# A two-layer decoder of mixers: gated linear attention ahead of latent attention, and the rotary table made between the two

## The chip, the core and the metric

The kernel runs on one core of one Trainium2 chip. The metric is the device time of one execution in microseconds. An execution has five engines with an instruction stream each: TensorE (PE, matrix products; PEld is its weight load), VectorE (DVE), ScalarE (ACT), GpSimd (POOL) and SyncE (SP, which issues DMAs). Matrix products write to PSUM, everything else lies in SBUF.

## The reference

Two layers act on x with 256 tokens of 1024 features. The first third of a layer is the part that the change touches: four mixers run on the same normalised input, and their outputs are gated and merged.

```python
def mixer_block(h, positions, w_in, ...):
    zin = h @ w_in
    (cq, ckv, kpe, sg_uv, gq, gk, gv, g_lr, g_og,
     dq, dk, dv, da, db, dz, gates) = jnp.split(zin, splits, axis=-1)
    o_a = mla_branch(cq, ckv, kpe, positions, mla_norm_q, mla_norm_kv, mla_w_uq, mla_w_ukv)
    o_b = spatial_gating_branch(sg_uv, sg_ln_g, sg_ln_b, sg_w, sg_b)
    o_c = gla_branch(gq, gk, gv, g_lr, g_og, gla_w_gate, gla_b_gate, gla_norm)
    o_d = deltanet_branch(dq, dk, dv, da, db, dz, dn_conv, dn_a_log, dn_dt_bias, dn_norm)
    proj = jnp.einsum('bsnw,nwd->bsnd', branches, w_branch)
    gate = jax.nn.sigmoid(gates).reshape(b, s, N_BRANCH, D_MODEL)
    return jnp.sum(gate * proj, axis=2) @ w_out
```

`mla_branch` (latent attention, MLA) normalises a compressed query and key, projects both up by weights of its own, rotates 32 of the features by the cosines and sines of the positions (the rotary table), and runs causal softmax attention with four heads. `gla_branch` (gated linear attention, GLA) weights the products of queries and keys by exponentials of summed log gates. `spatial_gating_branch` is gMLP, `deltanet_branch` DeltaNet. GLA and DeltaNet end in the same way: a norm of the heads' outputs, times a gate. After the mixers, a layer has cross-attention with a memory and an MLP, which the change leaves alone.

## The kernel before

**Weights.** All weights come as one stream from HBM in the order of use. A *half* is 128 x 1024 numbers. `half()` (line 174) takes the next one from a raw tile `wr` (three of them, filled by SP's DMAs with two halves each) and splits it into a high part `wh`, rounded to fp32r, on ACT (L191) and the remainder `wl` on DVE (L194). There are four tiles each for `wh` and `wl`. `mm3` (L198, L199, L200) makes one product out of three matmuls: high by high, low by high, high by low. A half feeds 24 matmuls of 256 columns, in groups of eight products that accumulate in a PSUM tile `g` (three of these).

**Order.** A list scheduler of the tile framework simulates the five engines when the kernel is built and fixes each engine's instruction stream. Among instructions that could start, the one earlier in the program goes first. The weight splits count as 200 places earlier than they stand, and statistics and the like as more. So the order in which the program text issues the mixers sets which DVE work competes with which split.

**The mixers.** In a layer the program first runs the input projection: five pairs of output blocks for DeltaNet's inputs and shared ones, then `soft_gates` and `conv` of DeltaNet, then `zin_rest` (four more pairs, and gMLP's and GLA's values by token). In layer 0, `rope_table` (L394) is called between `conv` and `zin_rest`. It loads the positions and the mask of GLA, multiplies the positions by frequencies on GpSimd (L400 to L404), takes off multiples of two pi on DVE (three times L410), folds (L412 on GpSimd, L414 and L415 on DVE) and takes the sine on ACT (L416) into a constant tile `cs`. Layer 1 uses the same `cs`.

Then two generators run in turns, a step of each at a time: `dn()`, which is DeltaNet's system, solve and output, and `others()`, which is gMLP, MLA and GLA in that order. Each `yield` in them ends a step. The program text of the gates (32 halves, their results in tiles `gt`) follows behind, and PE gets gate matmuls wherever the mixers leave room.

MLA (L897 to L1003) uses two halves of the weight stream of its own: the query's up-projection, 24 matmuls whose results are multiplied by `cs` on DVE (`qm`, L929), and the key's and value's. Its norm's root is some dozen steps of 0.15 us on DVE (`rsqrt`, L271 to L283). GLA (L789 to L893) makes differences `dd` of the summed gates at seven levels (DVE, L819 to L826), clamps them on GpSimd (L827), takes exponentials on ACT, multiplies 4 x 7 times a query by one of these (`qt`, DVE, L861), has PE multiply the result with keys (L866), and picks the masked entries into `sc` (DVE). Its values then enter by L885 to L888.

`head_out` (L754) is the end of DeltaNet and of GLA. It squares the output on ACT, sums on PE (L763), gates on ACT and DVE (L764 to L766), takes a reciprocal root of 14 steps on DVE, copies it out to `rb` on ACT (L779), transposes that on PE (L783), and multiplies (L784). It reads the gate into the tile of the squares, so the gate follows the sums.

**Tiles.** Mixers and others share a list of equal pieces in SBUF. `new` takes the piece that has been free longest, `rel` gives it back; a tile thereby waits for the last reader of the piece's former tile. The first four gate pairs have tiles of their own; from the fifth on (`m >= 4`) `gates` takes pieces.

Of the kernel before, what the change touches and what calls it, by code (L numbers as in the profile page):

```python
# [64 lines left out]
def decoder(ctx: ExitStack, tc: tile.TileContext, ws, xn_d, xt_d, mem_d, pos_d, fin_d, par_d, cst_d, msk_d, out_d):  # L65
# [29 lines left out]
    def new(dt=F32, shape=(P, 2, T), name="a"):  # L95
        assert free, "no piece left: " + str(sorted(n for _, _, n in owner.values()))
        i = free.pop(0)
        t = ap.tile(list(shape), dt, tag=f"pc{i}", name=nm(name))
        owner[id(t)] = (i, t, name)
        return t  # L100

    def rel(*ts):
        for t in ts:
            if isinstance(t, (list, tuple)):
                rel(*t)
                continue
            free.append(owner.pop(id(t))[0])
# [4 lines left out]
    def small2(a, b, name):  # L112
        return sp.tile([P, a, b], F32, tag=name, name=nm(name))

    def bank(shape=(P, 2, T)):
        return pp.tile(list(shape), F32, tag="s", name=nm("ps"))
# [3 lines left out]
    msk = cp.tile([P, M_N], I32, name="msk")  # L120
# [14 lines left out]
    def later(*a):  # L135

        tc.keep_in_program_order(nc.sync.dma_start(*a))
# [133 lines left out]
    def rsqrt(src, n, scale, eps, name):  # L271
        x = small(n, name + "x")
        y = small(n, name + "y")
        t = small(n, name + "t")
        V.tensor_scalar(x, src, scale, eps, op0=ALU.mult, op1=ALU.add)
        V.tensor_scalar(y.bitcast(I32), x.bitcast(I32), 1, None, op0=ALU.logical_shift_right)
        V.tensor_scalar(y.bitcast(I32), y.bitcast(I32), -1, MAGIC, op0=ALU.mult, op1=ALU.add)
        V.tensor_scalar(x, x, -0.5, None, op0=ALU.mult)
        for _ in range(3):
            V.tensor_tensor(t, y, y, op=ALU.mult)  # L280
            V.tensor_tensor(t, t, x, op=ALU.mult)
            V.scalar_tensor_tensor(y, t, 1.5, y, op0=ALU.add, op1=ALU.mult)
        return y  # L283
# [106 lines left out]
    def bc2(row, n=2):  # L390
        return row.unsqueeze(1).to_broadcast([P, n, T])


    def rope_table():  # L394
        posi = new(dt=I32, shape=(P, T), name="posi")
        later(posi, pos_d)
        later(msk, msk_d)
        ang, n = new(shape=(P, T)), new(shape=(P, T))
        q = slice(64, 128)
        G.tensor_copy(ang[q], posi[q])  # L400
        G.tensor_scalar(ang[q], ang[q], cst[q, C_FREQ : C_FREQ + 1], None, op0=ALU.mult)
        G.tensor_scalar(n[q], ang[q], float(1.0 / (2 * np.pi)), None, op0=ALU.mult)
        G.tensor_scalar(n[q], n[q], 12582912.0, None, op0=ALU.add)
        G.tensor_scalar(n[q], n[q], -12582912.0, None, op0=ALU.add)  # L404
        rest = 2 * np.pi
        for bits in (8, 8, 24):
            e = int(np.floor(np.log2(rest))) - bits + 1
            c = float(np.floor(rest / 2.0**e) * 2.0**e)
            rest -= c
            V.scalar_tensor_tensor(ang[q], n[q], -c, ang[q], op0=ALU.mult, op1=ALU.add)  # L410
        pi = float(np.nextafter(np.float32(np.pi), np.float32(0)))
        G.tensor_scalar(ang[q], ang[q], pi, -pi, op0=ALU.min, op1=ALU.max)  # L412
        c = slice(64, 96)
        V.scalar_tensor_tensor(ang[c], ang[c], -1.0, ang[c], op0=ALU.mult, op1=ALU.min)  # L414
        V.tensor_scalar(ang[c], ang[c], float(np.pi / 2), None, op0=ALU.add)  # L415
        S.activation(cs[q], ang[q], AF.Sin)  # L416
        G.memset(cs[0:64], 1.0)
        rel(posi, ang, n)

    def hsl(h):  # L420
        return slice(64 * (h % 2), 64 * (h % 2) + 64)
# [3 lines left out]
    def bch(a, shape=W4):  # L425
        return a.unsqueeze(1).to_broadcast(list(shape))
# [11 lines left out]
    def layer(l):  # L438
        pr = cp.tile([P, PC_N], F32, tag="par", name=nm("par"))

        def col(o, n=1):
            return pr[:, o : o + n]
# [7 lines left out]
        def out_branch(n, src):  # L450
            brh[n], brl[n] = new(F32R, name="brh"), new(F32R, name="brl")
            S.copy(brh[n], src)
            V.tensor_tensor(brl[n], src, brh[n].bitcast(F32), op=ALU.subtract)
# [284 lines left out]
        def zin_rest():  # L738
            def ev_rest(p, parts):
                ps = parts[0][1]  # L740
                t = new(name=("og", "dz", "cq", "su")[p])
                V.tensor_tensor(t, ps, bc2(R.rrow), op=ALU.mult)
                setattr(R, ("og", "dz", "cq", "su")[p], t)

            gemm(X, XL, 8, 4, ev_rest)
            R.zs = []

            def ev_tok(t, ps):
                z = new(name="zs", shape=(P, 512))
                S.activation(z, ps, AF.Copy, scale=R.rs[:, t : t + 1])  # L750
                R.zs.append(z)

            weights("tok")
            gemm_tok(X, XL, 8, ev_tok)  # L754
# [250 lines left out]
        def gmlp():  # L1005
            su, zs = R.su, R.zs

            def gelu2(z, shape):

                w = new(name="ge", shape=shape)  # L1010
                S.activation(w, z, AF.Square)
                G.tensor_scalar(w, w, 0.044715, 1.0, op0=ALU.mult, op1=ALU.add)
                G.tensor_tensor(w, w, z, op=ALU.mult)
                S.activation(w, w, AF.Tanh, scale=float(np.sqrt(2.0 / np.pi)))
                V.scalar_tensor_tensor(w, w, 1.0, z, op0=ALU.add, op1=ALU.mult)
                return w

            bst, bag = small2(2, 6, "bst"), small2(2, 2, "bag")
            vl = new(name="vl")
            gv = [gelu2(zs[t][:, 0:256], (P, T)) for t in range(2)]  # L1020
            for t in range(2):
                V.bn_stats(bst[:, t], gv[t])
                V.bn_aggr(bag[:, t], bst[:, t])
            rv = rsqrt(bag[:, :, 1], 2, 0.25, EPS, "ln")
            V.tensor_scalar(rv, rv, 0.5, None, op0=ALU.mult)
            for t in range(2):
                V.tensor_scalar(vl[:, t], gv[t], bag[:, t, 0:1], rv[:, t : t + 1], op0=ALU.subtract, op1=ALU.mult)
            rel(gv)
            G.tensor_tensor(vl, vl, bc2(col(PC_LNG, T)), op=ALU.mult)
            G.tensor_tensor(vl, vl, bc2(col(PC_LNB, T)), op=ALU.add)  # L1030
            yield
            wm = new(name="wm", shape=W4)
            G.tensor_tensor(wm, col(PC_WS, 512).rearrange("p (a b) -> p a b", a=4), bch(tri), op=ALU.mult)
            gu = gelu2(su, (P, 2, T))
            yield
            mp = bank()
            for h in range(4):
                for t in range(2):
                    PE.matmul(mp[hsl(h), h // 2, 128 * t : 128 * t + 128], vl[:, t, 64 * h : 64 * h + 64], wm[:, h], start=True, stop=True)
            mx = new(name="mx")  # L1040
            for t in range(2):
                s = slice(128 * t, 128 * t + 128)
                V.tensor_tensor(mx[:, :, s], mp[:, :, s], col(PC_BS, 256).rearrange("p (a b) -> p a b", a=2), op=ALU.add)
            V.scalar_tensor_tensor(mx, mx, 0.5, gu, op0=ALU.mult, op1=ALU.mult)
            out_branch(1, mx)
            rel(mx, gu, su, vl, wm)
            yield
# [6 lines left out]

        def others():
            yield from gmlp()
            yield from mla()
            yield from gla()

        soft_gates()  # L1060
        conv()
        if l == 0:
            rope_table()
        zin_rest()

        if l == 0:
# [3 lines left out]
        for j in range(4):  # L1070
# [7 lines left out]
            rel(t)  # L1078

        run = [dn(), others()]  # L1080
        while run:
            for gen in list(run):
# [208 lines left out]
    for l in range(NL):  # L1291
        layer(l)
# [177 lines left out]
```

## Time and profile before

| | before |
|---|---|
| median of 3 runs | 1099.93 us (1099.71 to 1100.56) |
| profiled execution, its own time | 1101.14 us |
| its span in the trace | 1098.5 us |
| mean granted TensorE clock | 0.996 |
| instructions | 20696 |

The span is the time from the first to the last instruction in the trace, and the remaining 2.6 us of the profiled execution lie around it. A group of instructions is printed as the line, the engine, the operation, the tile written and those read, the shape and the count; behind the bar stand the busy time in us and the mean of one in ns, then idle time of the engine ahead of it and what ended that. A wait is printed as who waited for whom, with the sum in us, the number of times and the longest. Layer 0's input projection runs until about 105 us of the span, its mixers until about 235 and its gates to the end of the mixers' third; layer 1's mixers begin at about 630 us.

### The profile page before, as it was taken

Reading aid. Unit: us, or ns where it says so; the run is one execution under the profiler, and the core shown is the slowest. Engines: PE = TensorE matmul, PEld = TensorE weight load, DVE = VectorE, ACT = ScalarE, POOL = GpSimd, SP = SyncE. Lnnn points to the kernel's source line nnn. Section 1 sums busy time; section 2 is a strip of 40 time slices with the busy share of each in tenths; the row PEclk is TensorE's granted clock in tenths of the full one; section 3 lists DMA queues with packets and bytes.
Section 4 is the critical chain, followed back from the end, with each engine's and each line's share of the span. In section 5 each row is a group of like instructions: output and inputs, shape, how many; then the busy total and the mean of one; then the engine's idle time right before and its main releaser. Section 6 shows DMA issues by size and latency. Waiting matters only on the chain.

```text
span 1098.5 us, 20696 instructions
## 1 busy us (share of the span) xinstructions
PE 1074.4 (98%) x8494; PEld 1032.4 (94%) x8494; DVE 812.5 (74%) x1419; ACT 584.2 (53%) x875; POOL 194.6 (18%) x170
## 2 busy tenths in 40 slices
PE   8989999999999999999999999999999999999996
PEld 8979998899998999999999899999999899999885
DVE  6999857779866876655679997686797768665454
ACT  6565554554645655544454746554455555555342
POOL 6234005108200200000101420320351001010000
PEclk9999999999999999999999999999999999999999
DMA  9442523354544455555545444244445345554551
GB/s 354 163 179 111 204 104 121 110 193 156 191 153 154 154 192 192 192 192 193 192 183 192 155 154 154 103 150 151 174 177 204 122 152 193 186 194 177 192 192 38
DMA packets 28319, 185.13 MB, mean 169 GB/s; under 512 B 3392, under 2 KB 3648, under 8 KB 6976
## 3 DMA queue, kind: packets, MB, share of 16 engines
q1 hardware_dynamic: 26208, 179.09, 44.9%
q10 hardware_dynamic: 2016, 4.72, 1.3%
q8 instruction: 66, 1.08, 0.4%
q14 instruction: 29, 0.24, 0.1%
HBM read 182.75 MB, written 1.05 MB: 167 GB/s over the span
## 4 chain that ended last, share of the span: by engine, by line
PE 86%; DVE 8%; ACT 2%; DMA 2%; issue 1%; POOL 0%; DVEq 0%; ACTq 0%
PE g L198 25%; PE g L199 25%; PE g L200 25%; DVE wl L194 2%; DMA mr<-memt 1%; PE ps L198 1%; PE ps L199 1%; PE ps L200 1%; ACT wh L191 1%; PE ps L666 1%; PE ps L662 1%; DVE cv L539 1%; DVE qt L861 0%; DMA wr<-ws 0%; PE ps L972 0%
## 5 line engine op out<-in xcount | busy, mean ns | idle before, releaser
L194 DVE TENSOR_TENSOR wl<-wr,wh 128x1024 fp32r<-128x1024 f32 (+1 forms) x337 | 416.9, 1239 | 187.8 <-ACT wh L191 186.6
L191 ACT ACTIVATE wh<-wr 128x1024 fp32r<-128x1024 f32 (+1 forms) x337 | 355.1, 1057 | 344.3 <-PE g L199 238.8
L200 PE MATMUL g<-hh,wl 128*128 128x256 f32 x1152 | 325.1, 282 | 3.5 <-DVE wl L194 3.5
L198 PE MATMUL g<-hh,wh 128*128 128x256 f32 x1152 | 323.8, 282 | 1.9 <-ACT gt L1097 1.4
L199 PE MATMUL g<-hl,wh 128*128 128x256 f32 x1152 | 322.9, 280 | 0.0
L200 PEld LDWEIGHTS g<-hh,wl 128*128 128x128 f32 x1152 | 216.5, 188 | 5.5 <-DVE wl L194 4.5
L198 PEld LDWEIGHTS g<-hh,wh 128*128 128x128 f32 x1152 | 216.5, 188 | 3.1 <-ACT gt L1097 1.8
L199 PEld LDWEIGHTS g<-hl,wh 128*128 128x128 f32 x1152 | 217.3, 189 | 0.4 <-issue 0.2
L338 POOL TENSOR_TENSOR sq<-sq,sq 128x512 f32<-128x512 f32 x14 | 21.2, 1513 | 350.5 <-ACT sq L330 350.3
L198 PE MATMUL g<-xh,wh 128*128 128x256 f32 x272 | 75.5, 281 | 2.0 <-ACT xh L311 2.0
L199 PE MATMUL g<-xl,wh 128*128 128x256 f32 x272 | 75.8, 281 | 0.0
L200 PE MATMUL g<-xh,wl 128*128 128x256 f32 x272 | 74.9, 280 | 0.0
L198 PE MATMUL g<-ah,wh 128*128 128x256 f32 x256 | 70.7, 276 | 0.0
L199 PE MATMUL g<-al,wh 128*128 128x256 f32 x256 | 70.7, 276 | 0.0
L200 PE MATMUL g<-ah,wl 128*128 128x256 f32 x256 | 70.7, 276 | 0.0
L198 PEld LDWEIGHTS g<-xh,wh 128*128 128x128 f32 x272 | 51.3, 190 | 2.4 <-ACT xh L311 2.4
L1113 POOL TENSOR_TENSOR gt<-gt,gt 128x512 f32<-128x512 f32 x16 | 35.6, 2228 | 91.0 <-DVE gt L1112 90.0
L199 PEld LDWEIGHTS g<-xl,wh 128*128 128x128 f32 x272 | 51.2, 189 | 0.1
L200 PEld LDWEIGHTS g<-xh,wl 128*128 128x128 f32 x272 | 51.0, 189 | 0.0
L200 PE MATMUL g<-wh,al 128*128 128x512 f32 x128 | 49.5, 389 | 0.0
L199 PE MATMUL g<-wl,ah 128*128 128x512 f32 x128 | 49.5, 389 | 0.0
L198 PE MATMUL g<-wh,ah 128*128 128x512 f32 x128 | 49.4, 390 | 0.0
(500 smaller groups left out, 2332.6 us busy)
## 6 DMA issues: line engine op xcount, KB each, us to landing
wr<-ws SPq DMA_DIRECT2D x166, 1024.0 KB, 4.8
wr<-ws ACTq DMA_DIRECT2D x4, 512.0 KB, 7.6
mr<-memt ACTq DMA_DIRECT2D x8, 256.0 KB, 4.5
par<-par SPq DMA_DIRECT2D x2, 778.0 KB, 7.0
x<-xt SPq DMA_DIRECT2D x3, 256.0 KB, 7.7
cst<-cst SPq DMA_DIRECT2D x1, 588.0 KB, 8.7
gf<-fin SPq DMA_DIRECT2D x2, 256.0 KB, 5.3
yt<-yg ACTq DMA_DIRECT2D x2, 256.0 KB, 2.5
```

What stands on the lines that cost most here:

```text
L191: i = S.activation(wh[:, p], r[:, p], AF.Copy)
L194: V.tensor_tensor(wl[:, p], r[:, p], wh[:, p].bitcast(F32), op=ALU.subtract)
L198: PE.matmul(out, ah, bh, start=start, stop=False)
L199: PE.matmul(out, ah, bl, start=False, stop=False)
L200: PE.matmul(out, al, bh, start=False, stop=stop)
L338: G.tensor_tensor(acc, acc, sq, op=ALU.add)
L539: V.scalar_tensor_tensor(cv[:, c, d], zc[p][:, c, 0 : T - 3 + k], col(o + k), cv[:, c, d], op0=ALU.mult, op1=ALU.add)
L662: PE.matmul(xp[:, h], M[:, h], Tm[:, h], start=True, stop=True)
L666: PE.matmul(up[:, h], X[t][:, h], U[:, h], start=True, stop=True)
L1113: G.tensor_tensor(gt[m][0], gt[m][0], gt[m][1], op=ALU.add)
```

## The change

GLA comes ahead of MLA in `others()`, in both layers. In layer 0 the rotary table is made between the two; the mask, which `rope_table` also loaded, is loaded where the table was made before. No step is added or left out.

```diff
@@ -394,7 +394,6 @@
     def rope_table():
         posi = new(dt=I32, shape=(P, T), name="posi")
         later(posi, pos_d)
-        later(msk, msk_d)
         ang, n = new(shape=(P, T)), new(shape=(P, T))
@@ -1054,13 +1053,15 @@
         def others():
             yield from gmlp()
+            yield from gla()
+            if l == 0:
+                rope_table()
             yield from mla()
-            yield from gla()
 
         soft_gates()
         conv()
         if l == 0:
-            rope_table()
+            later(msk, msk_d)
         zin_rest()
```

Lines from 398 to 1056 have numbers smaller by one in the changed kernel.

On DVE, between the splits of two neighbouring gate halves of layer 0 while DeltaNet's system is being solved (`w` is the solve, `rmt` MLA's norm, `wl` a split), there stood before:

```order
L194 TENSOR_TENSOR wl_1967<-wr_1936,wh_1966 128x1024
L642 TENSOR_TENSOR w_1111<-w_1111 128x8x13
L281 TENSOR_TENSOR rmt_1143<-rmt_1143,rmx_1141 128x4
L194 TENSOR_TENSOR wl_2000<-wr_1997,wh_1999 128x1024
L640 STREAM_SHUFFLE w_1111<-w_1111 128x8x12
L282 SCALAR_TENSOR_TENSOR rmy_1142<-rmt_1143,rmy_1142 128x4
```

And now, between the same two splits:

```order
L194 TENSOR_TENSOR wl_1967<-wr_1936,wh_1966 128x1024
L641 TENSOR_TENSOR w_1094<-w_1094 128x8x14
L452 TENSOR_TENSOR brl_1091<-mx_1086,brh_1090 128x512
L860 TENSOR_TENSOR qt_1240<-dd_1124,qbd_1118 128x128 x2
L860 TENSOR_TENSOR qt_1240<-dd_1124,qbd_1119 128x128 x2
L860 TENSOR_TENSOR qt_1263<-dd_1124,qbd_1118 128x128 x2
L860 TENSOR_TENSOR qt_1263<-dd_1124,qbd_1119 128x128 x2
L194 TENSOR_TENSOR wl_2000<-wr_1997,wh_1999 128x1024
```

Eight of GLA's multiplications have moved in between the two splits, and the small steps of MLA's norm have left.

On PE, at the end of DeltaNet's output in layer 0 (`ps_1628` takes the transposes of DeltaNet's `rb`, `ps_1643` and those after it GLA's products), there stood before:

```order
L200 MATMUL g_2545<-hh_930,wl_2577 128x256
L783 MATMUL ps_1628<-cst,rb_1626 128x128 x4
L866 MATMUL ps_1643<-qt_1638,kt_1478 128x256 x2
L866 MATMUL ps_1653<-qt_1648,kt_1479 128x256 x2
L866 MATMUL ps_1663<-qt_1658,kt_1479 128x256 x2
```

And now the last gate matmuls and both groups of transposes, followed by MLA's statistics (`sqk`, `sq`) and its keys (`ktr`):

```order
L199 MATMUL g_2423<-hl_914,wh_2454 128x256
L200 MATMUL g_2423<-hh_913,wl_2455 128x256
L782 MATMUL ps_1508<-cst,rb_1506 128x128 x4
L782 MATMUL ps_1520<-cst,rb_1518 128x128 x4
L904 MATMUL ps_1551<-cst,sqk_1548 128x1
L905 MATMUL ps_1551<-cst,sq_1547 128x1
```

Thirteen matmuls ahead of the first of these transposes, of the same gate tile, stand the two groups of four L762 (L763 before), one for each head output. The end of GLA has moved beside that of DeltaNet, and MLA behind both.

On DVE there now stand, between those two statistics and the transposes in layer 0, the roots of both outputs (`dn` and `gl`) step by step in turns, with the table's last steps (`a`) among them:

```order
L281 TENSOR_TENSOR dnt_1464<-dnt_1464,dnx_1462 128x8
L413 SCALAR_TENSOR_TENSOR a_1532<-a_1532 32x256
L281 TENSOR_TENSOR glt_1491<-glt_1491,glx_1489 128x8
L282 SCALAR_TENSOR_TENSOR dny_1463<-dnt_1464,dny_1463 128x8
L414 TENSOR_SCALAR a_1532<-a_1532 32x256
L282 SCALAR_TENSOR_TENSOR gly_1490<-glt_1491,gly_1490 128x8
```

Before, only one of the two roots was under way at a time, and the table's steps stood in the projection.

## The prediction

> **What bounds the kernel now.** I read the page's first lines and its chain first.
>
> ```profile
> span 1098.5 us, 20696 instructions
> PE 1074.4 (98%) x8494; PEld 1032.4 (94%) x8494; DVE 812.5 (74%) x1419; ACT 584.2 (53%) x875; POOL 194.6 (18%) x170
> PE 86%; DVE 8%; ACT 2%; DMA 2%; issue 1%; POOL 0%; DVEq 0%; ACTq 0%
> ```
>
> PE is idle for 1098.5 - 1074.4 = 24.1 us of the whole span. The change removes no matmul, so it can only fill idle time of PE or make more of it: each microsecond that PE waits anew is one on the clock. Next come the windows around the mixers of layer 0 (columns: PE, PEld, DVE, ACT, POOL busy, clock, DMA share, GB/s) and one of layer 1.
>
> ```profile
> 60.00:75.00 15.00, 13.95 (x72) 11.34 (x71) 14.88 (x17) 9.18 (x13) 3.79 (x3) 1.00 0.52 198
> 75.00:90.00 15.00, 11.94 (x95) 11.01 (x94) 14.57 (x38) 9.97 (x16) 6.56 (x6) 1.00 0.45 163
> 222.00:246.00 24.00, 24.00 (x207) 24.00 (x206) 19.48 (x45) 12.00 (x16) 0.00 (x0) 1.00 0.61 209
> 616.00:630.00 14.00, 13.08 (x113) 12.14 (x112) 11.90 (x33) 11.56 (x31) 7.06 (x9) 1.00 0.37 139
> ```
>
> From 60 to 90, while the last input projections run, DVE is busy 29.45 of 30 us and PE waits 1.05 + 3.06 = 4.1 us: here DVE is the bound. Where gates alone run (222:246), a matmul takes 24.0/207 = 0.116 us, so the 24 matmuls of one weight half take 2.8 us. What PE waits for there is the DVE half of the weight split; the first two rows are of the waits from 40 to 172, the last from 560 to 720:
>
> ```profile
> PE g L200 <- DVE wl L194: 2.6, 3, 0.9
> PE g L199 <- DVE wl L194: 1.0, 2, 0.7
> PE g L200 <- DVE wl L194: 0.9, 1, 0.9
> ```
>
> The table has its own time of 1101.14 us against a median of 1099.93: the profiled execution is 1.21 us above the runs, and the sum below is taken off both alike. A difference of 0.2%, 2.2 us, is about what a measurement of this kernel can tell from no change.
>
> **The change part by part.** These are the groups of DVE that the change moves, with busy time and mean ns of one:
>
> ```profile
> L410 DVE SCALAR_TENSOR_TENSOR a<-a,a 64x256 f32<-64x256 f32 x3 | 1.4, 450 | 0.1
> L414 DVE SCALAR_TENSOR_TENSOR a<-a 32x256 f32<-32x256 f32 x1 | 0.4, 416 | 0.0
> L415 DVE TENSOR_SCALAR a<-a 32x256 f32<-32x256 f32 x1 | 1.3, 1262 | 0.0
> L825 DVE TENSOR_TENSOR dd<-cum 128x128 f32<-128x128 f32 x14 | 5.0, 354 | 1.5 <-ACT cum L796 1.5
> L826 DVE TENSOR_TENSOR dd<-cum 128x128 f32<-128x128 f32 x14 | 3.9, 282 | 0.0
> L820 DVE TENSOR_SCALAR dd<-cum 128x128 f32<-128x128 f32 x2 | 1.2, 621 | 0.0
> L819 DVE COPY dd<-cum 128x128 f32<-128x128 f32 x2 | 0.4, 215 | 0.0
> L842 DVE COPY dg<-ps 128x8 f32<-128x8 f32 x2 | 0.3, 154 | 0.0
> L929 DVE TENSOR_TENSOR qm<-ps,cs 128x512 f32<-128x512 f32 x4 | 2.7, 678 | 0.0
> L320 DVE SCALAR_TENSOR_TENSOR cql<-cq,par,cqh 128x256 fp32r<-128x256 f32 x4 | 2.4, 589 | 0.0
> L281 DVE TENSOR_TENSOR rmt<-rmt,rmx 128x4 f32<-128x4 f32 x6 | 0.9, 150 | 0.0
> L642 DVE TENSOR_TENSOR w<-w 128x120 f32<-128x120 f32 (+14 forms) x30 | 9.3, 310 | 0.5
> ```
>
> 1. *The rotary table leaves the projection.* Its three L410, L414 and L415 take 1.4 + 0.4 + 1.3 = 3.1 us off DVE between 40 and 105, where DVE is full. PE's wait of 4.1 us there can fall by between 0 and 3.1; since DVE has next to no gap, I take 3.0. The position DMA, on SP's queue, moves behind the later weight loads; it is awaited by nothing before the table is made. The mask's DMA stays in its place. The six GpSimd steps go along; POOL is busy 10.35 of the 30 us, so their absence costs or brings nothing.
>
> 2. *GLA's preparation comes ahead of the weight splits.* I summed DVE's and PE's instructions in their new order, each at its mean duration in the trace, and compared the sums at each half's split. In layer 0 DVE is furthest behind PE shortly after DeltaNet's solve begins. By then DVE has done for GLA 7 x 0.354 + 7 x 0.282 for the decay differences, 0.62 + 0.22 + 0.15 for the three single steps, and 20 multiplications L861. Rows for those, beside no GpSimd step and beside some:
>
> ```profile
> 721.02 0.89 DVE L861 TENSOR_TENSOR qt<-dd,qbd 128x128 f32<-128x128 f32 x4
> 710.74 2.71 DVE L861 TENSOR_TENSOR qt<-dd,qbd 128x128 f32<-128x128 f32 x8
> ```
>
> One takes 0.22 to 0.34 us; I take 0.23, as most will run where POOL does little, so 4.6 us, and for GLA 2.5 + 2.0 + 1.0 + 4.6 = 10.1 us. Not done by then are the table (3.1), MLA's two L929 (1.4) and two L320 (1.2), 13 small steps of its norm's root at 0.15 (2.0), and seven steps of the solve, such as L642, with the shuffle and product that go with it just under its 0.31 (1.9). DVE has 10.1 - 9.6 = 0.5 us more to do. PE has 24 matmuls less to cover it, since MLA's queries, which stood there, come later: 2.8 us. Before, DVE's excess by the same sum is 3.8 us at its greatest and 3.0 at this half; PE's measured wait is 4.1, so the sum can be trusted to some tenths. After it is 3.0 + 0.5 + 2.8 = 6.3, by the sum in full (with each duration unrounded) 6.8. The net of points 1 and 2 is 6.8 - 3.8 = **+3.0 us**: the relief of 3.0 is spent and as much again.
>
> In layer 1 there is no table to leave. GLA's 10.1 us replace 1.4 + 1.2 + 2.0 + 1.9 = 6.5, so DVE has 3.6 more (4.0 unrounded), and PE 24 matmuls and a little less, 3.1 us. By the sum DVE was 1.3 us ahead of PE at this half and 0.9 behind at its worst, where PE waited 0.9; after it is 4.0 + 3.1 - 1.3 = 5.8 behind: **+4.9 us**. At 0.34 for the multiplications 20 x 0.11 = 2.2 us come on top, in each layer. It can be nothing at all if the order of the gates gives PE something else to do, but an engine's stream is fixed and the next gate needs the next half.
>
> [...] The traces of L861 and of GpSimd's clamp:
>
> ```profile
> L861 DVE TENSOR_TENSOR qt<-dd,qbd x56: 276/280/1125, 176.9 to 724.4; 128x128 f32<-128x128 f32 x56
> 172.38 7.35 POOL L827 TENSOR_SCALAR dd<-dd 128x512 f32<-128x512 f32 x4 [19.33 <-DVE dd L826]
> ```
>
> [...]
>
> 3. *Two head outputs end together in layer 0.* DeltaNet's output, and GLA's, wait for a chain: statistics on PE (L763), a gate and a reciprocal root on DVE, a copy on ACT, and transposes on PE (L783). All four of before:
>
> ```profile
> 190.81 0.95 PE L763 MATMUL ps<-cst,sq 128*128 128x2 f32 x8
> 202.38 0.66 PE L783 MATMUL ps<-cst,rb 128*128 128x128 f32 x4 [0.31 <-ACT rb L779]
> 220.32 0.95 PE L763 MATMUL ps<-cst,sq 128*128 128x2 f32 x8
> 231.94 0.60 PE L783 MATMUL ps<-cst,rb 128*128 128x128 f32 x4
> 726.61 0.95 PE L763 MATMUL ps<-cst,sq 128*128 128x2 f32 x8
> 737.82 0.66 PE L783 MATMUL ps<-cst,rb 128*128 128x128 f32 x4 [0.44 <-ACT rb L779]
> 756.33 0.95 PE L763 MATMUL ps<-cst,sq 128*128 128x2 f32 x8
> 767.95 0.60 PE L783 MATMUL ps<-cst,rb 128*128 128x128 f32 x4
> ```
>
> From start to start they take 11.57, 11.62, 11.21 and 11.62 us, and PE waited 0.31 and 0.44 of it in two of them, the rest being covered by gates. In the new order of layer 0 both statistics stand in a row, then 13 gate matmuls (13 x 0.116 = 1.5 us), then both groups of transposes. PE's stream does not hold another gate before them: from the fifth gate pair on, the result tiles reuse pieces that the head outputs have to free first. So PE waits 11.5 - 0.95 - 0.95 - 1.5 = **8.1 us**. DVE's own work bounds it from above: two heads' roots, their gating, the table's last steps and the weight splits between, with ACT's two table loads for the sine:
>
> ```profile
> 73.74 1.28 ACT L416 ACT_TABLE_LOAD   x1 [0.21 <-DVE a L415]
> 75.04 0.41 ACT L416 ACTIVATE cs<-a 64x256 f32<-64x256 f32 x1
> 75.47 1.28 ACT L1014 ACT_TABLE_LOAD   x1
> L194 DVE TENSOR_TENSOR wl<-wr,wh 128x1024 fp32r<-128x1024 f32 x3 | 3.7, 1225 | 3.5 <-ACT wh L191 3.5
> ```
>
> The last row is of 190:203: three splits, 3.7 us, were queued inside the chain of before. Without them it is 8.1 - 3.7 = 4.4 us; with them and both loads (2.6 us) and nothing saved 8.1 + 2.6 = 10.7. I keep 8.1: the splits go, but the second head's steps come. The sine starts 0.02 us after its load has ended (73.74 + 1.28 = 75.02). [...]
>
> In layer 1 three gate tiles, 144 matmuls or 16.7 us, stand between the two statistics and the transposes: nothing waits, and the wait of 0.44 goes. In layer 0 that of 0.31 is part of the 8.1. Together **-0.7**.
>
> The sum is 3.0 + 4.9 + 8.1 - 0.7 = 15.3 us: 1101.14 + 15.3 = 1116.4 profiled, 1099.93 + 15.3 = **1115.2 us** in the runs.
>
> **The rivals.** *Half of it* (0.17): the heads' chain is what its steps need, 4.4 us, and in layer 1 half the excess is absorbed: 3.0 + 2.5 + 4.4 - 0.7 = 9.2, so 1109. For it speaks that a waiting PE lets splits run ahead; against it that there are now two heads in the chain.
>
> *Faster* (0.10): the projection's relief decides. DVE keeps the 3.0 us that it gains, the splits stay ahead since DVE's later stretches have gaps (19.48 of 24 us busy in 222:246), and the heads hide: 1099.93 - 3.0 - 0.7 = 1096.2. It decides once the new waits stay under 3.7 us in all; the single row of 13 gate matmuls against an 11 us chain speaks against it.
>
> *No change* (0.07): new waits of some 4 us, the heads' 4.4 at their lowest and none elsewhere, pay for the same relief: 1099.93 + 4.4 - 3.7 = 1100.6. The scheduler then would have moved gates, not added waits.
>
> [...]
>
> **How the numbers follow.** The forecast has the remaining 0.60. Its own ends are 1115.2 + 2.6 + 2 x 2.2 = 1122.2 above and 1115.2 - 3.7 - 4.9 = 1106.6 below, where layer 1 absorbs all. The range goes from 1100 to 1123: it holds the forecast with both ends, the half and the case of no change, and leaves out the faster one and the blocked port, 0.16. Faster 0.10, same 0.07, slower 0.83.
>
> **What would show it.** Right: PE busy close to 15 in 75:90; more wait of PE on L194 between 100 and 140 in layer 0 and 640 to 680 in layer 1; a wait of some 8 us at the first transposes (L783, now L782) of layer 0, ended by ACT's copy of rb, and none in layer 1. Wrong: transposes that wait under 4 us, or L194 waits no longer than before; then the sums at mean durations have missed what DVE gains elsewhere. [...]

## The result and the profile after

The changed kernel takes 1131.99 us (median of 3 runs, 1131.90 to 1133.74) against 1099.93 before: a ratio of 1.0295, with a 95% interval of 1.0272 to 1.0319. It is slower by 32 us where 15 were forecast, and lies above the range. The first lines of the page after, with the row of the granted clock (tenths, 40 slices of 28 us):

```profile
span 1130.1 us, 20710 instructions
PE 1086.8 (96%) x8494; PEld 1042.5 (92%) x8494; DVE 812.7 (72%) x1419; ACT 582.1 (52%) x875; POOL 198.3 (18%) x170
PEclk9999999799999999999999999999999999999999
```

The span is 31.6 us longer. PE's idle time went from 24.1 to 1130.1 - 1086.8 = 43.3 us, that is 19.2 more. The other 12.4 us are in its busy time: 8494 matmuls as before, 1086.8 us in place of 1074.4. So two things happened, and the prediction has only the first. These are the main waits of PE (40:172 and 172:260, layer 0, then 560:720, layer 1):

```profile
PE g L200 <- DVE wl L194: 6.9, 3, 5.2
PE ps L847 <- POOL gks L835: 3.1, 1, 3.1
PE ps L559 <- DVE g L521: 1.0, 1, 1.0
PE ps L1038 <- POOL vl L1029: 0.2, 1, 0.2
...
PE ps L782 <- ACT rb L778: 9.4, 1, 9.4
...
PE g L200 <- DVE wl L194: 7.6, 5, 3.7
```

And the windows around four of these waits (columns as before: PE, PEld, DVE, ACT, POOL busy, granted clock, DMA share, GB/s):

```profile
104.00:110.00 6.00, 0.79 (x5) 0.59 (x4) 6.00 (x17) 3.13 (x5) 6.00 (x4) 0.85 0.00 1
110.00:116.00 6.00, 5.84 (x31) 5.54 (x30) 6.00 (x18) 1.65 (x3) 3.78 (x7) 0.58 0.51 175
...
122.00:126.00 4.00, 4.00 (x21) 3.95 (x21) 0.25 (x1) 0.00 (x0) 0.00 (x0) 0.60 0.27 111
194.00:204.00 10.00, 0.64 (x6) 0.44 (x5) 7.53 (x34) 4.14 (x6) 1.09 (x2) 0.65 0.35 132
204.00:214.00 10.00, 10.00 (x46) 9.82 (x47) 6.71 (x21) 6.18 (x11) 2.47 (x4) 0.50 0.08 26
214.00:224.00 10.00, 10.00 (x86) 10.00 (x86) 5.89 (x8) 6.36 (x11) 1.64 (x2) 1.00 0.37 134
678.00:682.00 4.00, 4.00 (x23) 4.00 (x21) 4.00 (x10) 0.65 (x3) 3.73 (x7) 0.57 0.00 0
```

Read the pairs: PE hardly works (it is busy for 0.79 of 6 us, and for 0.64 of 10), and in the window behind it PE is busy nearly throughout, the granted clock is 0.58 and 0.50, and about half as many matmuls fit: 46 in 10 us, then 86. From 209 to 214 a matmul of 256 columns starts every 0.213 us; it is 0.116 in the gates. Counted as length times what is missing from a clock of 1, the four stretches lose 2.5 us (110:116), 1.6 (122:126), 5.0 (204:214) and 1.7 (678:682), 10.8 in all. Such a stretch is called a dip below. The kernel before had one at its start alone, 3.4 us at a clock of 0.50 or 1.7 us lost (the idle last microseconds of both kernels aside), and the changed one's profile has none there: a net 9.1 of the 12.4.

The heads' chain itself, the two groups of four statistics and of four transposes in layer 0:

```profile
191.07 1.84 PE L762 MATMUL ps<-cst,sq 128*128 128x2 f32 x16
203.91 1.97 PE L782 MATMUL ps<-cst,rb 128*128 128x128 f32 x8 [9.36 <-ACT rb L778]
```

### The profile page after: what moved, and what is told of

It is laid out like the page before. It is cut to its first block, busy times and chain, and to the rows that moved or that the text cites. A ratio compares the mean times of both kernels' runs of the same rounds, so it can differ in the third digit from the quotient of the medians.

```text
span 1130.1 us, 20710 instructions
## 1 busy us (share of the span) xinstructions
PE 1086.8 (96%) x8494; PEld 1042.5 (92%) x8494; DVE 812.7 (72%) x1419; ACT 582.1 (52%) x875; POOL 198.3 (18%) x170
## 4 chain that ended last, share of the span: by engine, by line
PE 84%; DVE 10%; ACT 2%; POOL 1%; issue 1%; DMA 0%; ACTq 0%; DVEq 0%; POOLq 0%
PE g L198 25%; PE g L199 25%; PE g L200 25%; DVE wl L194 3%; PE ps L198 1%; PE ps L865 1%; PE ps L199 1%; PE ps L200 1%; DVE qt L860 1%; ACT wh L191 1%; PE ps L665 1%; PE ps L661 1%; DVE dd L825 1%; POOL ge L1011 0%; DMA wr<-ws 0%
## 5 line engine op out<-in xcount | busy, mean ns | idle before, releaser
L194 DVE TENSOR_TENSOR wl<-wr,wh 128x1024 fp32r<-128x1024 f32 (+1 forms) x337 | 414.3, 1232 | 205.7 <-ACT wh L191 204.1
L200 PEld LDWEIGHTS g<-hh,wl 128*128 128x128 f32 x1152 | 219.1, 190 | 17.0 <-DVE wl L194 16.7
L198 PEld LDWEIGHTS g<-hh,wh 128*128 128x128 f32 x1152 | 219.1, 190 | 1.5 <-ACT gt L1098 0.8
L199 PEld LDWEIGHTS g<-hl,wh 128*128 128x128 f32 x1152 | 220.0, 191 | 0.3
```

The source lines that it names most:

```text
L194: V.tensor_tensor(wl[:, p], r[:, p], wh[:, p].bitcast(F32), op=ALU.subtract)
L198: PE.matmul(out, ah, bh, start=start, stop=False)
L199: PE.matmul(out, ah, bl, start=False, stop=False)
L200: PE.matmul(out, al, bh, start=False, stop=stop)
```

## Experiments

The theory formed from these traces, theory 1 in the expectations: new waits of PE, from GLA's early steps and the joint chain, and behind each longer wait a stretch at half clock. Theory 2: the clock dips are a state of the chip and have nothing to do with the waits. Theory 3: the table's new place is the cost.

**The change in parts.** `swap_only` leaves the table in the projection:

```diff
             yield from gla()
-            if l == 0:
-                rope_table()
             yield from mla()
...
         if l == 0:
+            rope_table()
             later(msk, msk_d)
```

> Only the mixers' order is changed in both layers; the table stays in the projection. In this order 96 gate matmuls (11 us) stand between the heads' statistics and their transposes in layer 0, not 13. Theory 1 (new waits of PE, and on top of each wait over some 3.5 us a stretch at half clock): the heads' wait of 9.4 us goes with the half-clock stretch of about 6 us behind it, the waits for weight splits stay, and the projection's relief of 3 us is lost: 1132 - 9.4 - 6 + 3 = 1120. Theory 2 (the clock dips are a state of the chip in that execution and have nothing to do with waits): 1132 - 9.4 + 3 = 1126, with a clock of about 0.985 again. Theory 3 (the table alone costs the time, its sine in the heads' chain): within 3 us of 1100.

It took 1120.95 us (ratio 1.0191, 1.0174 to 1.0208), as theory 1 has it. PE's waits in layer 0 from 40 to 172:

```profile
PE g L198 <- ACT wh L191: 5.3, 2, 4.5
PE g L200 <- DVE wl L194: 4.9, 3, 2.3
```

No wait for `rb` is left in that layer. The waits for splits are there without the table's move, most of them now for the high part, which ACT makes. The table's move on top of the swap costs 11.0 us (1131.99 - 1120.95): in the traces 13 matmuls stand between the heads' statistics and their transposes in layer 0 with it, and 96 without it, so the heads' wait comes with the table.

`table_only` moves the table and keeps GLA last (against the kernel before):

```diff
             yield from gmlp()
+            if l == 0:
+                rope_table()
             yield from mla()
             yield from gla()
...
         if l == 0:
-            rope_table()
+            later(msk, msk_d)
```

> Only the table is moved, ahead of MLA; GLA stays last in both layers. Theory 1: no wait of GLA's kind and no joint chain, so 1097 to 1100, the projection's relief of up to 3 us, clock 0.996 or more. Theory 3 (the table's place costs): 1110 or more, with the wait on ACT around the sine.

Measured: 1106.43 us, 1.0057 (1.0042 to 1.0072). Both expectations miss it. Its waits from 40 to 105 and from 172 to 222:

```profile
PE ps L916 <- POOL ktr L914: 1.8, 1, 1.8
PE g L200 <- DVE wl L194: 1.3, 2, 0.9
PE ps L618 <- DVE dec L598: 1.0, 1, 1.0
...
PE ps L706 <- DVE s L703: 2.5, 1, 2.5
```

The projection's relief is real: L194 and `dec` cost 2.3 us there where 4.1 were lost before. But the sine now comes just ahead of MLA's keys, and PE's stream waits 1.8 us for `ktr`, which needs it. Its windows behind that wait and behind the one for `s`:

```profile
102.00:108.00 6.00, 4.34 (x18) 4.17 (x19) 6.00 (x18) 1.21 (x3) 2.48 (x3) 0.59 0.01 3
178.00:184.00 6.00, 3.54 (x15) 3.25 (x16) 4.25 (x18) 2.29 (x4) 6.00 (x5) 0.51 0.34 141
```

PE is busy 1079.1 us in this kernel, 4.7 more than before, and idle 1104.8 - 1079.1 = 25.7, 1.6 more. So the waits ate up the relief, and the clock behind the two longest (6 x 0.41 + 6 x 0.49 = 5.4 us) cost three times what the idle time grew by.

`swap_layer0` and `swap_layer1` change the order in one layer alone. The first has the table moved; the second has `l == 1` in the two new places, and leaves the table in the projection:

```diff
-            yield from gla()
+            if l == 0:
+                yield from gla()
             if l == 0:
                 rope_table()
             yield from mla()
+            if not (l == 0):
+                yield from gla()
```

> The changed kernel in layer 0, the former order in layer 1. Theory 1: layer 1's share is its L194 waits, 7.6 against 0.9 us, some 2 us of half clock, less the two waits of 1.2 us that the new order had covered: 7 to 8 us. So 1124 to 1125. Theory 2: 1125 to 1126.

> The former kernel in layer 0, GLA first in layer 1 only. Theory 1: the 7 to 8 us of layer 1 alone: 1107 to 1108, the clock dip of about 4 us at half speed behind a wait for L194 between 670 and 690. Theory 2 has no dip at that place.

They took 1121.61 us (1.0190, 1.0175 to 1.0205) and 1111.45 (1.0096, 1.0076 to 1.0116; single runs from 1107.95 to 1113.19). The excesses over before, 21.4 and 11.2, add up to 32.6, the whole change's 32.1 within the intervals: the two layers' costs add. Layer 1's share was expected at 7 to 8, so both runs miss their expectations. In the profile of `swap_layer1` the wait for `gks`, which the whole change has only in layer 0, stands in layer 1 as well:

```profile
PE ps L847 <- POOL gks L835: 2.8, 1, 2.8
```

**The clock.** `filler` gives PE needless matmuls in the heads' wait:

```diff
+N_FILL = 20
...
+            if l == 0 and name == "gl":
+                f = small(8, "fill")
+                V.tensor_copy(f, flat(st))
+                fp = bank()
+                for i in range(N_FILL):
+                    PE.matmul(fp[0:8, i % 2], f, cst[:, 0:T], start=True, stop=True)
             yield
             rb = new(name="rb", shape=(P, 8, 64))
```

> The changed kernel with 20 needless matmuls (128x256, f32, 0.43 us each) on PE in the heads' wait of layer 0; nothing reads them. Theory 1 (a long wait halves PE's clock afterwards): PE is not idle, so the 10 us at half clock behind the transposes run at full clock and some 5 us are won by more work: 1126 to 1128. Theory 2 (the dips have nothing to do with waits): 1132 or a little more, clock 0.984.

It took 1126.28 us (1.0239, 1.0220 to 1.0257), 5.7 us less than the changed kernel with 8.8 us more of PE work, as theory 1 has it. Theory 2 falls. The first of MLA's products in the changed kernel, and in `filler`:

```profile
209.31 0.41 PE L199 MATMUL ps<-cql,wh 128*128 128x256 f32 x1
209.52 0.41 PE L200 MATMUL ps<-cqh,wl 128*128 128x256 f32 x1
```

```profile
192.73 8.80 PE L782 MATMUL ps<-cst,fill 128*8 128x256 f32 x40
202.35 1.18 PE L789 MATMUL ps<-cst,rb 128*128 128x128 f32 x8 [0.82 <-ACT rb L785]
205.25 0.28 PE L200 MATMUL ps<-cql,wh 128*128 128x256 f32 x1
205.37 0.28 PE L201 MATMUL ps<-cqh,wl 128*128 128x256 f32 x1
```

The same matmuls start every 0.21 us in the one and every 0.12 in the other.

`gaps` measures the clock by itself:

```python
for n in (1, 2, 3, 4, 5, 6, 8, 10, 14, 18, 10, 8, 6, 5, 4, 3, 2, 1, 6, 6, 4, 4):
    # 140 matmuls of PE; then n + 1 steps of DVE and one of ACT, on which the next 140 depend
```

> Leaves out the decoder: 140 dense fp32r matmuls of 256 columns, a wait of PE for a chain of DVE steps of chosen length, and so 22 times; the output is a copy of x. Theory 1: waits under 2 us leave the granted clock at 1.0; from about 4 us on it is 0.5 when the matmuls start again, and for 4 us or more after that. Theory 2: no relation of the clock to the length of the wait.

Of its 22 stretches, the start, the length and the wait ahead of some:

```profile
44.61 17.05 PE L32 MATMUL ps<-a 128*128 128x256 f32 x140 [1.62 <-ACT a L38]
128.86 18.55 PE L32 MATMUL ps<-a 128*128 128x256 f32 x140 [3.08 <-ACT a L38]
151.15 19.41 PE L32 MATMUL ps<-a 128*128 128x256 f32 x140 [3.74 <-ACT a L38]
294.53 17.05 PE L32 MATMUL ps<-a 128*128 128x256 f32 x140 [3.09 <-ACT a L38]
377.39 18.55 PE L32 MATMUL ps<-a 128*128 128x256 f32 x140 [1.77 <-ACT a L38]
```

A stretch takes 17.05 us at full clock. Waits of 1.29, 1.44 and 1.62 us leave it so. From 3.74 us on, each costs 1.2 to 2.5 us more. In between, nine of twelve waits had a dip: 1.77 had one, and 3.08 had one, but the three of 3.09 had none. In the decoder a wait of 3.6 us (`light_dd`, layer 1) had one, a clock of 0.50 from 672 to 674, and one of 3.4 (`own43`, layer 0) had none, 1.00 throughout. So the expectation's limits were too neat: a wait of the same length may cost its length or 1.5 us more.

Where the wait lies decides it, and the records of the granted clock in the sixteen packed traces show how. They change only on a grid of 3.413 us: in the changed kernel 30, 32, 34, 35, 56, 61, 197, 198 and 328 times that length behind the first record. The grid's place differs from trace to trace: one of its points lies 0.78 us behind the span's start in the kernel before, 2.35 in the changed one. Of the 4888 grid intervals that began at full clock, the 66 in which PE idled for 1.86 us or more were all followed by one at half clock; of the 4810 with less than 1.7 us, six were; of the twelve between, five. In the two kernels' own traces the intervals ahead of a dip held 1.97, 2.36, 2.77, 2.80 and 3.41 us of idle PE, and the fullest of the others 1.54. The 1.77 us lie in one interval (374.98 to 378.39). The 3.09 us ahead of 294.53 are cut into 1.61 and 1.47 by the grid. A wait of 3.74 us, however it is cut, leaves some 1.87 us in one interval, which fits the waits that always had a dip.

A dip ends on the same grid. Of 74 intervals at half clock with less than 0.6 us of idle PE, 62 were the last of their dip; the other twelve all lie behind a wait for `rb`, in seven kernels. In the changed kernel that dip runs on to 214 although PE is busy from 204 on: transposes and MLA's statistics (128x1) stand at its head, and it ended only in MLA's products. Why these intervals did not end it is not shown.

**The heads' wait.** `pieces48` has `N_PIECE = 48` for 44:

> The changed kernel with 48 pieces in place of 44. 104 gate matmuls (12 us) then stand between the heads' statistics and transposes in layer 0, not 13. Theory 1 (the reuse of pieces keeps the gates back): the wait of 9.4 us and the 5 us lost to half clock behind it go: 1117 to 1119. Theory 3 (the chain of roots, sine and copies is the cost whatever PE has to do): PE waits for rb as before, 1130 to 1133.

It took 1127.08 us (1.0241, 1.0220 to 1.0262). The wait for `rb` in layer 0 is gone, so it was the reuse of pieces that kept the gates back; but only 5 us are won, not 14. PE's idle time is 1126.1 - 1084.6 = 41.5 us, against 43.3. Waits came up elsewhere, here in layer 1 (7.6 us in the changed kernel):

```profile
PE g L200 <- DVE wl L194: 8.9, 4, 5.3
```

The likely reading is that gates which PE does in one place cover nothing in another. As a control, `before_pieces48` has the same edit in the kernel before:

> The kernel before with 48 pieces. Its heads' chains are covered already (waits of 0.3 and 0.4 us), so freeing gates wins nothing there: 1098 to 1101. If pieces were short in this order too, 1096 or less.

1101.01 us, 1.0009 (1.0000 to 1.0019): nothing to win there.

**The waits for splits.** `slots5` has five tiles each for `wh` and `wl` (`bufs=5` for 4):

> The changed kernel with five tiles each for wh and wl in place of four. DVE then has three more splits ahead of GLA's differences. Theory 1a (MLA's two halves, split early and used late, hold two of the four tiles, so that no split can run ahead of GLA's steps): the L194 waits of 6.9 us in layer 0 and 7.6 in layer 1 fall below 3 each, and the clock dips behind them go: 1132 - 9 - 5 = 1118. Theory 1b (DVE simply has too much to do there): waits move but stay, 1129 to 1133.

1132.63 us (1.0295, 1.0276 to 1.0313). L194's waits came to 5.0 us in layer 0 (6.9 before the edit) and 4.4 in layer 1 (7.6): smaller, not gone, and other waits took the rest, as theory 1b has it. `light_dd` takes the differences off DVE and leaves GLA's decays out:

```diff
-                        V.tensor_tensor(d3[:, :, 0], ref, c3[:, :, 0], op=ALU.subtract)
-                        V.tensor_tensor(d3[:, :, 1], c3[:, :, 1], ref, op=ALU.subtract)
+                        S.copy(d, cum)
```

> The changed kernel without GLA's 28 two-sided differences on DVE (L824, L825, 12.9 us in both layers); ACT copies the summed gates in their place, so GLA's decays are left out of the computation. If GLA's DVE steps are what the splits wait for: the L194 waits of 6.9 us in layer 0 and 7.6 in layer 1 fall to 2 or less each, and the clock dips behind them (some 4 us lost at 108 to 115 and 678 to 682) go: 1132 - 11 - 4 = 1117. If the tiles held by MLA's halves make the wait whatever DVE does: 1128 or more.

1124.54 us (1.0225, 1.0207 to 1.0242), between the two expectations. Its waits from 40 to 172, and from 560 to 720:

```profile
PE g L200 <- DVE wl L194: 3.7, 3, 2.0
PE g L198 <- ACT wh L191: 3.2, 2, 1.7
...
PE g L200 <- DVE wl L194: 5.5, 4, 3.6
```

`own43` gives MLA's two halves tiles of their own, and has 43 pieces for 44 to make room (the lines that choose the tiles, cut):

```diff
-            wh, wl = (wp.tile([P, 1024 + SLACK // 4], F32R, tag=n, name=nm(n), bufs=4) for n in ("wh", "wl"))
+            wh, wl = (wp.tile([P, m], F32R, tag=n + k, name=nm(n)) for n in ("wh", "wl"))
```

> The changed kernel with split tiles of their own for MLA's two halves, so that all four shared ones serve the gates; 43 pieces in place of 44 to make room. No gate matmul stands before the heads' transposes in layer 0 then, so that wait is 11 us or more in place of 9.4, and is not counted. If MLA's held tiles make the L194 waits: layer 0's 6.9 and layer 1's 7.6 us fall to 2 or less each. If GLA's DVE steps make them whatever the tiles: 5 or more each.

L194's waits fell to 3.7 us in layer 0 and 2.8 in layer 1, no dip is left behind them, and the time stays at 1132.92 (1.0297, 1.0273 to 1.0321), since the heads now wait 7.5 + 2.3 us in layer 0 and 3.1 in layer 1. Both falls lie between the two expectations: neither cause alone is all of it. The split between them is not exact, for the differences took less in `own43` too, 9.8 us of DVE in place of 12.9. `light_own43` has both edits:

> own43 with ACT's copies in place of GLA's 28 two-sided differences (the decays are left out of the computation). If held tiles and GLA's DVE steps together make the L194 waits: under 1.5 us in each layer. If there is a third cause: 2.5 or more in one of them. The heads' waits stay as in own43, so the time says little: 1122 to 1132.

Its waits for splits, 40 to 172 and 560 to 720:

```profile
PE g L206 <- DVE wl L200: 1.8, 2, 1.4
...
PE g L206 <- DVE wl L200: 1.0, 1, 1.0
```

1.8 and 1.0 us of 6.9 and 7.6, a little above the 1.5 expected in layer 0: the two causes together are nearly all. The time is 1118.54 us (1.0167, 1.0138 to 1.0197), below the 1122 to 1132 expected.

`ks_first` computes `gqe` and `gks` ahead of the `kt` on GpSimd:

> The changed kernel with GpSimd's two last products, gqe and gks, ahead of the seven kt. PE's wait of 3.1 us for gks in layer 0 goes, and with it the dip to half clock at 122 to 126 that costs 1.7 us. If PE is the bound there: 1127. If DVE is the bound right after it, and PE only waits elsewhere: 1130 to 1133.

1130.92 us (1.0277, 1.0259 to 1.0295), a miss of its own aim: PE still waits 2.6 us for `gks`. ACT's last exponential comes as late as before (115.74 us after 115.79), and the first GpSimd product behind it takes 2.94 us, and `gks` 1.43, where such a product takes 0.5 elsewhere. DVE runs twelve of GLA's multiplications and two splits at that time. So it is in each place where PE waits long for `gks`: the first GpSimd product behind the last exponential takes 2.80 us in layer 0 of the changed kernel and of `swap_layer0`, and 5.04, 3.06 and 3.06 in `pieces48` (layer 0), `filler` and `swap_layer1` (layer 1). In layer 1 of the changed kernel and in layer 0 of `filler` it takes 0.54 us, and there is no such wait. DVE runs a row of multiplications there, too, but more slowly: in the changed kernel eleven take 3.10 us in layer 1, where twelve take 2.50 in layer 0.

**A try at the kernel before.** `before_idle10` has `N_IDLE = 10` for 6:

> The kernel before with 10 needless products at its start in place of 6, 0.43 us each, which fill the wait of 2 us for the first operands; no other line differs. In the profile of before, 3 us behind this wait ran at half clock. If a filled wait keeps the clock, 0 to 2 us are won, most in executions that had the dip: 1098 to 1100. If not, 1100 to 1101.

1101.82 us, 1.0017 (1.0008 to 1.0026), above both expectations. The dip at the start is gone, but another appeared at 76 to 82, where PE is idle for 1.5 us in both kernels: the grid of the clock lies otherwise. In `before_idle10` one interval (74.10 to 77.52) holds 1.85 us of idle PE, in the kernel before the two at this place hold 0.63 and 1.02. The window 8:10 and this one, in `before_idle10`, then in the kernel before:

```profile
8.00:10.00 2.00, 2.00 (x18) 1.91 (x17) 1.62 (x3) 1.86 (x3) 1.35 (x2) 1.00 1.04 411
76.00:82.00 6.00, 4.55 (x25) 4.56 (x26) 5.60 (x11) 2.62 (x6) 5.76 (x5) 0.72 0.46 175
```

```profile
8.00:10.00 2.00, 2.00 (x10) 1.87 (x10) 1.61 (x3) 1.85 (x4) 1.24 (x2) 0.50 1.02 411
76.00:82.00 6.00, 4.47 (x34) 4.08 (x35) 5.57 (x15) 5.04 (x8) 2.76 (x4) 1.00 0.53 186
```

No kernel tried here beats the one before.

## Why the prediction was wrong

The sign, the places of the waits and the heads' chain were right. The step that failed is the first: "each microsecond that PE waits anew is one on the clock". A longer wait costs its length and then the half clock behind it: at the heads 9.4 us, and 5.0 more. The waits forecast, 15.3 us, compare with 19.2 us measured; the 12.4 us of slower matmuls had no term at all. With the waits as measured and no slower matmul, the time would be 1099.93 + 19.2 = 1119.1 us, inside the range. The granted clock stood in every row of windows that was quoted, always at 1.00, but no single wait in those stretches was over 1 us. The term was not weighed, with a wait of 8.1 us forecast: in `gaps` each wait from 3.74 us on had its dip, and so had nine of the twelve from 1.77 to 3.09.

Point by point:

1. *The table leaves the projection*, -3.0 us. PE's waits from 40 to 105 fell from 4.1 to 2.7 us in the changed kernel and to 2.3 of its kind in `table_only`: 1.4 to 1.8, inside the bounds of 0 and 3.1. What the step did not price is what waits for the sine in its new place: 1.8 us for `ktr`, and the dip behind it, in `table_only`. "Their absence costs or brings nothing" held for GpSimd, not for who needs the table.

2. *GLA's preparation ahead of the splits*, net +3.0 and +4.9 us. Measured: PE's waits from 40 to 172 rose from 4.1 to 11.2, +7.1, and layer 1's from 0.9 to 7.9 (L194 and one of 0.3), +7.0. The mechanism was right, the size too small. The sum over both streams lets DVE fall behind as long as the totals agree; it takes the reserve of split halves as given. But MLA's halves are split early and held until MLA runs, so two of the four tiles are out and the reserve is what the other two hold, 2 x 2.8 = 5.6 us of PE. In layer 0 DVE's two splits around the differences start 9.0 us apart:

```profile
99.21 1.22 DVE L194 TENSOR_TENSOR wl<-wr,wh 128x1024 fp32r<-128x1024 f32 x1
108.20 1.21 DVE L194 TENSOR_TENSOR wl<-wr,wh 128x1024 fp32r<-128x1024 f32 x1
```

And on ACT in layer 1 the next `wh` (the last row) stands behind gMLP's output, which waits for the same stretch of DVE:

```profile
674.92 0.62 ACT L451 CAST brh<-mx 128x512 fp32r<-128x512 f32 x1 [3.16 <-DVE mx L1043]
675.97 1.04 ACT L191 ACTIVATE wh<-wr 128x1024 fp32r<-128x1024 f32 x1
```

`own43` and `light_dd` show that the held tiles and GLA's steps both matter, `light_own43` that together they are nearly all of the waits for splits. Of the 7.1 us in layer 0, 3.1 are PE's wait for `gks` on GpSimd, which the prediction did not have.

3. *The heads' chain*, +8.1 us: 9.36 measured, between the 8.1 and the 10.7 given. The sine's load (1.28 us) and the sine (0.41) did stand ahead of both copies, and the second load behind them. The sine began 0.02 us after its load had ended (201.51 + 1.28 = 202.79, and 202.81), as before. That PE had nothing else because of the pieces is shown by `pieces48`. That a gate covers only once is what the step, and the expectation of `pieces48`, left out. The step also read the order of layer 1 wrongly: 96 matmuls stand there between the statistics and the transposes, 11.1 us, not 144. They still cover the chain.

4. *The waits that go*, -0.7: those from 172 to 222 were 4.5 us before and are 2.1 beside the heads' now, and layer 1's 1.2 us from 720 to 780 are gone, so -3.6. 7.1 + 7.0 + 9.4 - 3.6 = 19.9 against the idle time's 19.2; 0.6 of the rest is less wait ahead of 40 us (2.7 for 3.3).

Of the rivals, the faster one and no change are excluded by the interval, and the half by its size. The 0.16 that the range leaves out hold 0.06 for a blocked port, multiplications that stand still while GpSimd clamps; no run shows that. They took 355 ns in the mean, less than the 390 before, and 632 ns at most (before: 276 at least, 280 in the median, 1125 at most). What took longer are the differences: 524 and 401 ns (282 and 354 before), two in each layer 1.13 to 1.15 us while GpSimd built `sc` (2.09 us from 101.44, 2.27 from 669.60), 14 x 0.242 + 14 x 0.047 = 4.0 us in all:

```profile
L825 DVE TENSOR_TENSOR dd<-cum 128x128 f32<-128x128 f32 x7 | 3.7, 525 | 0.0
L824 DVE TENSOR_TENSOR dd<-cum 128x128 f32<-128x128 f32 x7 | 2.8, 401 | 0.0
```

These are layer 0's, from 100 to 110. And beside the multiplications it is GpSimd that took longer: its first two products behind the last exponential took 2.80 and 1.43 us in layer 0, 0.54 and 0.50 in layer 1, and only layer 0 has the wait of 3.1 us for `gks`. No run takes the multiplications away there: that they are the cause is the author's estimate from the six places named at `ks_first`, and no run shows how.

What stays open: of the 12.4 us more of PE's busy time, 3.3 were not located; and since the place of the clock's grid differs from trace to trace, which wait between 1.8 and 3.4 us gets a dip can't be foretold from these runs.

## What to carry to other kernels

Price a new wait of PE, where PE is the bound as here, in two parts, its length and what PE does at half clock behind it; a forecast wait of several microseconds needs that second term, here 12.4 us beside 19.2, two thirds of the first. When an order of work moves, ask which buffers the displaced step now holds longer, for a reserve of four tiles with two of them out is a reserve of two. Work that covers a wait is spent once: filling one gap with gates opened another, while matmuls that nobody reads won 5.7 us.

## What the runs showed of the hardware

The granted clock changed on a grid of 3.413 us: half an interval of idle PE (1.86 us or more) was enough to halve it for the next interval, in all 66 cases of the sixteen traces. In the changed kernel it went from 1.0 to 0.5 2.4 us after PE went idle (194.6 to 196.9), and it came back 3 to 10 us after work began again. A wait of 1.77 us had a dip and three of 3.09 us had none, so executions of one and the same program may differ by some us: `swap_layer1` ran between 1107.95 us, at a mean granted clock of 0.996, and 1113.19 us, at 0.991, and 0.005 of 1111 us is 5.6 us where the two differ by 5.2. The kernel before has a dip at its start, behind an interval with 1.97 us of idle PE, while the changed kernel has none at the same place, with 1.34 us. In each layer of the changed kernel two of GLA's differences on DVE took four times their time, 1.13 to 1.15 against 0.28 us, while GpSimd built `sc`, and GpSimd's products took 2.80 to 5.04 us for 0.5 beside a row of GLA's multiplications on DVE.
